# Turning half of the scan's output and half of the attention norm's state by transposing DMA reads instead of TensorE

## The chip, the cores and the metric

One Trainium2 chip, one core. The metric is the device time of one execution in microseconds, taken as the median of the runs.

## The reference

One layer of a hybrid decoder trunk over 256 tokens of width 2048: a half-step SwiGLU, a projection that feeds a gated group and a Mamba-2 scan, an output projection of both, cross-attention to 256 memory tokens, a second half-step SwiGLU and a final norm. The change touches the scan's output on its way into the output projection, and the state `h` on its way into the attention's query projection:

```python
h = h + 0.5 * swiglu(rmsnorm(h, ffn1_norm), ffn1_w_gu, ffn1_w_down)
proj = rmsnorm(h, mix_norm) @ w_in
gu, gv, z, xbc, dt_raw = split(proj)
a_out = chunked_sgu(gelu(gu), gelu(gv), gm_v_norm, gm_w_s, gm_b_s)
m_out = mamba2_group(z, xbc, dt_raw, ...)      # rmsnorm(y * silu(z), ssm_norm)
h = h + concat([a_out, m_out]) @ w_out
h = h + memory_cross_attention(rmsnorm(h, xa_norm), rmsnorm(mem, mem_norm), w_q, w_kv, w_o)
h = h + 0.5 * swiglu(rmsnorm(h, ffn2_norm), ffn2_w_gu, ffn2_w_down)
return rmsnorm(h, final_norm)
```

## The kernel before

**Products.** All large products run on TensorE as three matmuls of a split: each float32 operand becomes a rounded part `hi` and a rest `lo`, and `hi*hi`, `hi*lo`, `lo*hi` are added in PSUM. Weights arrive from HBM in blocks of 256 rows by two times 512 columns (`raw`, three buffers, L147). ACT casts a block to `hi` (L193, three buffers), DVE subtracts to `lo` (L201, two buffers). The activations are stored with features across the partitions, so that tokens have to be turned into that form first.

**Plain and summed blocks.** A plain block ("C") takes 24 matmuls of 512 columns. A summed block ("S") computes the 2 x 2 product by seven products instead of eight: 21 matmuls, for which DVE first makes four sums of the weights (`sum`, L201), ACT casts and DVE splits those too. Which block is which stands in strings such as `OUT_KINDS = "CCCCSCSC", "SCSCSCSC"`.

**The output projection** (`add_sum` with `w_out`) goes over all 16 blocks for the first two 512-column pieces of `h` (`h0`, `h1`), then over 16 blocks for the other two. In the first half blocks 0 to 5 and 7 are plain and 6 is summed, then S and C alternate from 8 to 15; in the second half blocks 0 to 3 are plain and then S and C alternate from 4. Blocks 0 to 7 multiply the gated group (`at`, `ats`), blocks 8 to 15 the scan's output (`mt`, `mts`). The scan's output has four quarters of 512 features, `c` = 0 to 3; quarter `c` gives an S piece (`mts`) and a C piece (`mt`), used by blocks 8 + 2c and 9 + 2c.

**Order.** TensorE's instructions keep the order in which the code writes them. Other work is put off with `later(fn, by)`, counted in steps, one per weight block (a C block counts as two halves). A put-off job that takes a PSUM bank is held back while summed blocks run; one marked `bankless` is not. Casts of weights stay in order among themselves on ACT, and so do the splits on DVE; a scheduler fits the other instructions between them.

**Turning on TensorE.** `m_operand(c)` scales quarter `c` of `y` by the norm's factor (L1051), one step after the other, and `mts.later` turns it a step later: per piece four transposes of 128 x 128 into a bank (`tpose`, L77). From the bank, ACT and DVE make the piece's forms: for a C piece two scaled casts on ACT (L435) and two rests on DVE (L438); for an S piece two scaled copies (`forms`, L526), three differences on DVE (L530, L532, L533), two casts (L535) and two rests (L536). `Normed.chunk(n)` does the same for the state's chunk `n` with the name `xp_xa`: all four pieces of chunks 0 and 1 are C pieces and are turned at the second half's first step.

**Turning by DMA.** Other operands of the kernel already take another way, `turn_over` (L390 to L397): ACT copies the 16-bit halves of each token row apart (`halves`), POOL's queue writes them to DRAM (`planes`), and two transposing reads on SP's queue bring 256 features by 256 tokens each into SBUF (`turned`), from where the same forms are made. With `lined=True` such a read is tied to the place between weight loads at which the code issues it (SP's queue runs in order), and both reads of a pair go at one place.

Of the kernel before, what the change touches and what calls it, by code (L numbers as in the profile page):

```python
# [34 lines left out]
KG = 4  # L35
# [4 lines left out]
C_FFN1, C_MIX, C_SSM, C_XA, C_MEM, C_FFN2 = (16 * i for i in range(6))  # L40
# [7 lines left out]
def hybrid_layer(ctx: ExitStack, tc: tile.TileContext, x, xt, mem, memt, w_gu1, w_dn1, w_in, w_s, w_out,  # L48
# [30 lines left out]
    def later(fn, by=1, bankless=False):  # L79
        put_off.append((steps[0] + by, len(put_off), fn, bankless))  # L80
# [363 lines left out]
    def operand_later(srcs, to, name, c0=None, by=1):  # L444
        def half(q):
            if q == 0:
                to.append(slot([P, KG, 2 * S], F32R, name))
            return to_operand(srcs, to[at], q, c0)

        at = len(to) + sum(1 for o in owed if o is to)  # L450
        owed.append(to)

        def first():
            owed.remove(to)
            assert len(to) == at
            half(0)
            later(lambda: half(2), by=0)

        later(first, by)

    def operand_turned(srcs, to, name, c0=None, by=(1, 4), lined=False):
        at = len(to) + sum(1 for o in owed if o is to)
        owed.append(to)

        def put(src, q):
            if q == 0:
                owed.remove(to)
                assert len(to) == at
                to.append(slot([P, KG, 2 * S], F32R, name))
            to_operand(src, to[at], q, c0)  # L470

        turn_over(srcs, by, put, lined)
# [77 lines left out]
    class Normed:  # L550
# [8 lines left out]
        def chunk(self, n, by=1):  # L559
            srcs = [h[n][:, t, :] for t in range(NT)]  # L560
            if n < 2 and not isinstance(self.xts, Pieces):
                operand_turned(srcs, self.xts, f"xt_{self.name}{n}", self.c0 + n * KG, (2.5 + 1.5 * n, 2.5))
                self.stats(n)
            elif isinstance(self.xts, Pieces):

                for i in (2 * n, 2 * n + 1):
                    later(lambda i=i: self.xts.put(i, srcs, i % 2 * KP, self.c0 + n * KG),
                          self.bys.get(i, by))
                later(lambda: self.stats(n), self.stats_by)
            else:  # L570
                operand_later(srcs, self.xts, f"xt_{self.name}{n}", self.c0 + n * KG, by)
                self.stats(n)
# [472 lines left out]
    mts = Pieces(OUT_KINDS[1], "mt")  # L1045

    def m_operand(c):
        gs = []
        for t in range(NT):
            ys = y[t][:, c * 8:c * 8 + 8, :].rearrange("p h d -> p (h d)")  # L1050
            nc.vector.tensor_scalar(out=ys, in0=ys, scalar1=rstd_m[:, t:t + 1], scalar2=None, op0=ALU.mult)  # L1051
            gs.append(ys)
        mts.later(gs, C_SSM + c * KG)

    for c in range(4):
        later(lambda c=c: m_operand(c), by=1 + c)
    na = Normed("xa", C_XA, XA_KINDS, {4: 1, 6: 1, 5: 1.5, 7: 2}, 8)

    class Both:
# [201 lines left out]
```

## Time and profile before

| what | value |
|---|---|
| median of 3 runs | 2417.68 us (2417.51 to 2418.0) |
| profiled execution, its own time | 2417.13 us |
| span of its instructions | 2415.4 us |
| mean granted TensorE clock | 0.999 |
| instructions | 29003 |
| moved by DMA | 523.80 MB, mean 217 GB/s |

A row of the timeline gives start and length in us, engine, line, operation, what it writes and reads, and how often; behind it, in brackets, the idle time of the engine before it and what ended that. Rows of a tile's view give shortest, median and longest duration in ns. A row of waits gives who waited for whom, the sum in us, how often, and the longest. Starts of consecutive matmuls tell more than their lengths, because matmuls overlap.

### The profile page before, as it was taken

Reading aid. Unit: us, or ns where it says so; the run is one execution under the profiler, and the core shown is the slowest. Engines: PE = TensorE matmul, PEld = TensorE weight load, DVE = VectorE, ACT = ScalarE, POOL = GpSimd, SP = SyncE. Lnnn points to the kernel's source line nnn. Section 1 sums busy time; section 2 is a strip of 40 time slices with the busy share of each in tenths; the row PEclk is TensorE's granted clock in tenths of the full one; section 3 lists DMA queues with packets and bytes.
Section 4 is the critical chain, followed back from the end, with each engine's and each line's share of the span. In section 5 each row is a group of like instructions: output and inputs, shape, how many; then the busy total and the mean of one; then the engine's idle time right before and its main releaser. Section 6 shows DMA issues by size and latency. Waiting matters only on the chain. (4 is left out here: it accounts for less than half of the span.)

```text
span 2415.4 us, 29003 instructions
## 1 busy us (share of the span) xinstructions
PE 2402.6 (99%) x11037; PEld 1999.1 (83%) x11037; DVE 2030.9 (84%) x1941; ACT 1385.1 (57%) x1286; POOL 85.3 (4%) x158
## 2 busy tenths in 40 slices
PE   9999999999999999999999999999999999999998
PEld 7888888888888888788888888888888888888887
DVE  8999889999877786655698988788799988999997
ACT  7566446656557664446555666655565654556554
POOL 1000000000001000000000010000000000000000
PEclk9999999999999999999999999999999999999999
DMA  8767667777757775567557677745677676677764
GB/s 307 236 220 235 207 203 232 222 225 234 242 186 215 217 227 177 202 199 227 191 192 240 230 244 226 228 157 173 201 224 232 218 223 200 219 233 222 234 219 154
DMA packets 294763, 523.80 MB, mean 217 GB/s; under 512 B 104016, under 2 KB 106096, under 8 KB 293856
## 3 DMA queue, kind: packets, MB, share of 16 engines
q1 hardware_dynamic: 283936, 485.82, 64.1%
q0 software_dynamic: 9856, 35.08, 3.9%
q8 instruction: 86, 1.41, 0.2%
q10 hardware_dynamic: 832, 1.05, 0.1%
q14 instruction: 53, 0.43, 0.0%
HBM read 476.76 MB, written 23.63 MB: 207 GB/s over the span
## 5 line engine op out<-in xcount | busy, mean ns | idle before, releaser
L201 DVE TENSOR_TENSOR lo<-raw,hi 128x2048 fp32r<-128x2048 f32 (+2 forms) x449 | 945.0, 2106 | 243.2 <-PE acc L74 170.3
L193 ACT CAST hi<-raw 128x2048 fp32r<-128x2048 f32 (+1 forms) x437 | 784.8, 1798 | 439.3 <-PE acc L74 378.9
L74 PE MATMUL acc<-hi,xp_ffn 128*128 128x512 f32 x1824 | 574.2, 389 | 0.0
L74 PEld LDWEIGHTS acc<-hi,xp_ffn 128*128 128x128 f32 x1824 | 342.4, 188 | 71.2 <-ACT hi L215 0.2
L193 ACT CAST hi<-sum 128x2048 fp32r<-128x2048 f32 x117 | 224.1, 1915 | 294.4 <-PE acc L74 148.1
L74 PE MATMUL acc<-lo,xp_ffn 128*128 128x512 f32 x912 | 355.1, 389 | 1.0 <-DVE h L682 0.9
L201 DVE TENSOR_TENSOR lo<-sum,hi 128x2048 fp32r<-128x2048 f32 x117 | 268.1, 2291 | 38.4 <-ACT hi L193 38.4
L74 PE MATMUL acc<-hi,hid 128*128 128x512 f32 x896 | 281.2, 389 | 0.0
L74 PE MATMUL acc<-hi,xt_mix 128*128 128x512 f32 x768 | 240.9, 392 | 0.0
L74 PEld LDWEIGHTS acc<-lo,xp_ffn 128*128 128x128 f32 x912 | 171.2, 188 | 37.4 <-DVE h L682 1.4
L621 DVE TENSOR_TENSOR part<-acc,part 128x512 f32<-128x512 f32 x272 | 179.9, 685 | 20.7 <-PE acc L74 7.0
L74 PEld LDWEIGHTS acc<-hi,hid 128*128 128x128 f32 x896 | 168.2, 188 | 34.9
L74 PE MATMUL acc<-lo,hid 128*128 128x512 f32 x448 | 174.3, 389 | 0.0
L74 PEld LDWEIGHTS acc<-hi,xt_mix 128*128 128x128 f32 x768 | 144.2, 188 | 30.8 <-issue 1.0
L201 DVE TENSOR_TENSOR sum<-sum,raw 128x512 f32<-128x512 f32 x234 | 161.6, 690 | 6.3
L74 PE MATMUL acc<-lo,xt_mix 128*128 128x512 f32 x384 | 149.5, 389 | 0.0
L74 PE MATMUL acc<-hi,xp_ffn1s 128*128 128x512 f32 x466 | 148.6, 389 | 0.0
L74 PE MATMUL acc<-hi,xp_ffn2s 128*128 128x512 f32 x466 | 148.6, 389 | 0.0
L201 DVE TENSOR_TENSOR sum<-raw 128x1024 f32<-128x1024 f32 x117 | 142.5, 1218 | 0.1
L74 PE MATMUL acc<-xt_mix,hi 128*128 128x512 f32 x512 | 140.1, 395 | 0.0
L74 PE MATMUL acc<-hi,hids 128*128 128x512 f32 x392 | 125.2, 389 | 0.0
L74 PE MATMUL acc<-hi,memt 128*128 128x512 f32 x384 | 121.4, 390 | 0.0
(291 smaller groups left out, 3183.3 us busy)
## 6 DMA issues: line engine op xcount, KB each, us to landing
raw<-in_w_gu SPq DMA_DIRECT2D x284, 512.0 KB, 4.6
raw<-in_w_in SPq DMA_DIRECT2D x80, 1024.0 KB, 5.2
raw<-in_w_dn SPq DMA_DIRECT2D x60, 1024.0 KB, 5.3
raw<-in_w_gu SPq DMA_DIRECT2D x136, 256.0 KB, 4.8
raw<-in_w_kv SPq DMA_DIRECT2D x24, 1024.0 KB, 5.9
raw<-in_w_out SPq DMA_DIRECT2D x21, 1024.0 KB, 5.3
planes<-halves POOLq DMA_DIRECT2D x74, 256.0 KB, 5.0
raw<-in_w_dn SPq DMA_DIRECT2D x28, 512.0 KB, 4.2
```

The costliest lines, as they stand in the source:

```text
L74: return pe(nc.tensor.matmul(out, lhsT=lhsT, rhs=rhs, start=start, stop=stop))
L193: last_cast[:] = [nc.scalar.copy(out=t[:, :n], in_=x[:, :n]).ins]
L201: last_split[:] = [nc.vector.tensor_tensor(**kw).ins]
L621: nc.vector.tensor_tensor(out=out, in0=a, in1=b, op=op)
```

## The change

Quarters 2 and 3 of the scan's output and chunks 0 and 1 of the state go the DMA's way. Their reads are tied to the order of weight loads. The four quarters are also scaled in another order of steps: 0, 2, 1, 3 at 1, 1.5, 2 and 2.5.

```diff
             if n < 2 and not isinstance(self.xts, Pieces):
                 operand_turned(srcs, self.xts, f"xt_{self.name}{n}", self.c0 + n * KG, (2.5 + 1.5 * n, 2.5))
                 self.stats(n)
+            elif n < 2 and self.name == "xa":
+                self.xts.turn_later(srcs, (5 + 1.5 * n, 1.5), self.c0 + n * KG, 2 * n, lined=True)
+                later(lambda: self.stats(n), self.stats_by)
             elif isinstance(self.xts, Pieces):
...
             gs.append(ys)
-        mts.later(gs, C_SSM + c * KG)
+        if c < 2:
+            mts.later(gs, C_SSM + c * KG)
+        else:
+            mts.turn_later(gs, (4.5, 1.4), C_SSM + c * KG, 2 * c, lined=True)

     for c in range(4):
-        later(lambda c=c: m_operand(c), by=1 + c)
+        later(lambda c=c: m_operand(c), by=(1, 2, 1.5, 2.5)[c], bankless=c > 1)
```

On TensorE, at the start of the output projection's second half, the sixteen transposes of `h0` and `h1` are gone (the groups of eight for `y` went in the same manner):

```order
 L74 MATMUL acc<-hi,at 128x512 x2
 L74 MATMUL acc<-lo,at 128x512
-L74 MATMUL acc<-hi,at 128x512
-L77 MATMUL tpose<-ident,h_90 128x128 x8
-L77 MATMUL tpose<-ident,h_91 128x128 x8
-L74 MATMUL acc<-hi,at 128x512
+L74 MATMUL acc<-hi,at 128x512 x2
 L74 MATMUL acc<-lo,at 128x512
```

The matmuls on both sides now follow each other.

On DVE, in the first half, from the sums of block 8 to the rest of block 9, there stood before only the splits of these two blocks:

```order
L201 TENSOR_TENSOR sum<-raw 128x1024
L201 TENSOR_TENSOR sum<-sum,raw 128x512 x2
L201 TENSOR_TENSOR lo<-raw,hi 128x1536
L201 TENSOR_TENSOR lo<-sum,hi 128x2048
L201 TENSOR_TENSOR lo<-raw,hi 128x2048
```

In the changed kernel the same stretch holds the last rest of quarter 2's S piece and most of quarter 3's work:

```order
L201 TENSOR_TENSOR sum<-raw 128x1024
L536 TENSOR_TENSOR mts<-forms,mts 128x512
L201 TENSOR_TENSOR sum<-sum,raw 128x512 x2
L201 TENSOR_TENSOR lo<-raw,hi 128x1536
L201 TENSOR_TENSOR lo<-sum,hi 128x2048
L530 TENSOR_TENSOR forms<-forms 128x256
L536 TENSOR_TENSOR mts<-forms,mts 128x512
L532 TENSOR_TENSOR forms<-forms 128x128
L438 SCALAR_TENSOR_TENSOR mt<-turned,col,mt 128x256
L533 TENSOR_TENSOR forms<-forms 128x128
L438 SCALAR_TENSOR_TENSOR mt<-turned,col,mt 128x256
L201 TENSOR_TENSOR lo<-raw,hi 128x2048
```

Quarter 2's other DVE work (one `mts` ahead of block 7's rest; behind it `forms`, `mt`, `forms`, `mt`, `forms`) stands just ahead of this piece. All of it stood among the sums and rests of block 6 before, with sources in PSUM (`tpose`).

On SP's queue, in the first half, the pairs of reads stand behind the loads of blocks 7 and 8:

```order
 L147 DMA raw<-in_w_out 128x512 x2
 L147 DMA raw<-in_w_out 128x2x1024
-L147 DMA raw<-in_w_out 128x2x512
-L147 DMA raw<-in_w_out 128x512 x2
+L147 DMA_TRANSPOSE turned<-planes 128x2x512 x2
+L147 DMA raw<-in_w_out 128x2x512
+L147 DMA raw<-in_w_out 128x512 x2
+L147 DMA_TRANSPOSE turned<-planes 128x2x512 x2
 L147 DMA raw<-in_w_out 128x2x1024
 L147 DMA raw<-in_w_out 128x2x512
```

The first pair fetches quarter 2, the second quarter 3. In the second half, chunk 0's pair stands behind the load of block 6 and chunk 1's behind that of block 8.

## The prediction

> **What bounds the kernel now.** I read the page's first part, then TensorE's waits over the whole span, then the timeline of the two places that the change touches.
>
> ```profile
> PE 2402.6 (99%) x11037; PEld 1999.1 (83%) x11037; DVE 2030.9 (84%) x1941; ACT 1385.1 (57%) x1286; POOL 85.3 (4%) x158
> PE acc L74 <- DVE lo L201: 1.3, 2, 0.9
> ...
> PE dt L74 <- issue: 0.5, 1, 0.5
> ```
>
> TensorE is busy for 2402.6 of 2415.4 us, and its waits, of which the first and the last of four rows stand above, sum to 4.0 us. A busy row alone proves little, because ends of matmuls are modelled, so the pitch between starts has to agree.
>
> ```profile
> 1213.05 0.39 PE L74 MATMUL acc<-hi,ats 128*128 128x512 f32 x1
> 1223.25 0.39 PE L74 MATMUL acc<-hi,mts 128*128 128x512 f32 x1
> 1228.01 0.39 PE L74 MATMUL acc<-hi,mt 128*128 128x512 f32 x1
> ```
>
> These are the first matmuls of weight blocks 6 (S, 21 matmuls), 8 (S) and 9 (C) of the output projection's first half, counted from 0; between 6 and 8 lies block 7 (C, 24 matmuls). 10.20 us over 45 and 4.76 over 21 is 0.227 us each, 5.44 for a C block, with no room for a wait. So time is TensorE's instructions at their pitch, plus whatever a change makes TensorE wait. An instruction removed from TensorE is worth its pitch; work on other engines costs nothing until a weight block's `hi` or `lo` comes late.
>
> **What the change removes.** 32 transposes leave TensorE: two groups of 8 for the scan's quarters 2 and 3, one of 16 for the state's chunks 0 and 1.
>
> ```profile
> 1200.16 0.39 PE L74 MATMUL acc<-hi,at 128*128 128x512 f32 x1
> 1200.39 1.03 PE L77 MATMUL tpose<-ident,y 128*128 128x128 f32 x8
> 1201.18 0.48 PE L74 MATMUL acc<-hi,ats 128*128 128x512 f32 x1
> 1201.49 0.40 PE L74 MATMUL acc<-lo,ats 128*128 128x512 f32 x1
> 1269.27 0.39 PE L74 MATMUL acc<-hi,at 128*128 128x512 f32 x1
> 1269.50 1.91 PE L77 MATMUL tpose<-ident,h 128*128 128x128 f32 x16
> 1271.16 0.48 PE L74 MATMUL acc<-hi,at 128*128 128x512 f32 x1
> 1271.47 0.39 PE L74 MATMUL acc<-lo,at 128*128 128x512 f32 x1
> ```
>
> From the matmul before a group to the second one behind it (the first one behind also starts its successor late) are 1201.49 - 1200.16 = 1.33 us where two pitches would be 0.45: 0.88 us for 8. In the large group it is 2.20 - 0.45 = 1.75 us for 16. Both give 0.11 us per transpose. The second group of 8 is alike, so the gain is 0.88 + 0.88 + 1.75 = **3.5 us**. Nothing else stands beside these instructions on TensorE, so all of it is on the path.
>
> The profile also shows the transposing op's own length, which is not its price here:
>
> ```profile
> L77 PE MATMUL tpose<-ident,h 128*128 128x128 f32 x80 | 10.5, 272 | 0.0
> ```
>
> The Trainium skill's page "VectorE: DVE Perf Modes", section "The three transpose paths", puts a 128x128 transpose at 390 ns on TensorE against 1309 ns through a DMA, and its rules tell the author to use TensorE where PSUM will do as the destination. Taken as prices on the path, its 390 ns would make the removal worth 12.5 us, an estimate from that page; taken as a rule, it speaks against the change. This trace disagrees with both uses: transposes overlap down to 0.11 us, and a DMA's length matters only if somebody waits for it.
>
> **What it adds off TensorE.** Each of four turn-overs needs two ACT copies into halves, two POOL writes to DRAM and two transposing reads on SP's queue.
>
> ```profile
> L390 ACT COPY halves<-gate x8: 1042/1048/1062, 1047.1 to 1098.0; 128x1024 uint16<-128x1024 uint16 x8
> planes<-halves POOLq DMA_DIRECT2D x74, 256.0 KB, 5.0
> L147 SPq DMA_TRANSPOSE turned<-planes x72: 1235/1289/4259, 61.1 to 2291.9; - x72
> turned<-planes SPq DMA_TRANSPOSE x72, 4.2
> 1186.82 2.47 DVE L1051 TENSOR_SCALAR y<-y,rstd_m 128x512 f32<-128x512 f32 x6 [0.82 <-POOL rstd_m L382]
> 1194.92 2.28 DVE L201 TENSOR_TENSOR lo<-raw,hi 128x2048 fp32r<-128x2048 f32 x1
> 1200.36 2.29 DVE L201 TENSOR_TENSOR lo<-raw,hi 128x2048 fp32r<-128x2048 f32 x1 [0.17 <-PE acc L74]
> ```
>
> ACT gains 8 x 1.05 = 8.4 us, and over the whole span it is idle for 43%; the casts behind the transposes stay, they only move. DVE's scalings of `y` come out every 0.4 us from 1186.8, quarter 2's as third and fourth, so ACT copies its halves from about 1188.2 to 1190.3, and with 5.0 us of landing and something for the issue the planes are there near 1196. SP reaches the reads behind block 7's load, which waits for block 4's `lo` (over at 1197.2 now; I allow it 0.7 more), at about 1198.4. They hold SP for 2 x 1.29 us and have landed by 1204; ACT wants them just ahead of block 7's `lo`, near 1210. Quarter 3's halves come one group later, near 1196, its planes near 1202; its reads follow block 8's load, which waits for block 5's `lo` (1202.7 now, about 1 more), near 1205, land near 1210.6 and are wanted behind block 8's sums, near 1221. I cost queue and landing at **0**: the cover is over 2 us ahead of each read and 6 us or more behind it. Gone, it would cost what the reads are late beyond it, one for one.
>
> **Where it does cost: DVE's order.** The work that turned pieces need on DVE (differences, `mts` and `mt` lows) moves from the time of the plain blocks 4 and 5, where DVE had room, to that of blocks 6 to 8, where S and C alternate and DVE is at its fullest. Its pitch is seen where it stands now, and DVE's full order without it in the rows that follow:
>
> ```profile
> 1209.31 0.41 DVE L530 TENSOR_TENSOR forms<-forms 128x256 f32<-128x256 f32 x1
> 1209.64 0.68 DVE L536 TENSOR_TENSOR mts<-forms,mts 128x512 fp32r<-128x512 f32 x1
> 1210.24 0.28 DVE L532 TENSOR_TENSOR forms<-forms 128x128 f32<-128x128 f32 x1
> 1210.44 0.47 DVE L438 SCALAR_TENSOR_TENSOR mt<-tpose,col,mt 128x256 fp32r<-128x256 f32 x1
> ...
> 1211.43 2.28 DVE L201 TENSOR_TENSOR lo<-sum,hi 128x2048 fp32r<-128x2048 f32 x1
> ...
> 1214.23 2.28 DVE L201 TENSOR_TENSOR lo<-raw,hi 128x2048 fp32r<-128x2048 f32 x1
> 1216.44 1.22 DVE L201 TENSOR_TENSOR sum<-raw 128x1024 f32<-128x1024 f32 x1
> 1217.69 1.42 DVE L201 TENSOR_TENSOR sum<-sum,raw 128x512 f32<-128x512 f32 x2
> 1219.02 1.75 DVE L201 TENSOR_TENSOR lo<-raw,hi 128x1536 fp32r<-128x1536 f32 x1
> 1221.16 2.29 DVE L201 TENSOR_TENSOR lo<-sum,hi 128x2048 fp32r<-128x2048 f32 x1 [0.39 <-ACT hi L193]
> 1223.37 2.29 DVE L201 TENSOR_TENSOR lo<-raw,hi 128x2048 fp32r<-128x2048 f32 x1
> ```
>
> By starts, the first six rows take 2.12 us; with the second `mts` (0.60, like the first) a quarter costs DVE 2.72 us. Both quarters now stand between `lo` of block 7 and `lo` of block 9, the latter quarter's last `mts` excepted. Count from the moment block 7's `lo` may start: only two such buffers exist, so it waits until block 5 is through, which is where block 6 starts, 1213.05 now and 1213.05 - 1.76 = 1211.3 without the two groups of 8. One `mts` (0.60, its cast ready at about 1211.4) stands ahead of it, so it starts at 1212.0 and DVE goes on at 1214.2. Then: quarter 2's five small ones, 0.33 + 2 x 0.40 + 2 x 0.20 = 1.53, to 1215.8; the block's first sum 1.25 (1216.44 to 1217.69) and `mts` 0.60, to 1217.6; the other sums 1.33, to 1218.9. From there to `lo<-sum` it is 2.14, with ACT's cast between: 1221.1, and on at 1223.3. Quarter 3's first six ops, 2.12, end at 1225.4, and `lo` of block 9 is ready 2.29 later, at 1227.7. TensorE needs it for the second matmul of block 9, at 1228.01 - 1.76 + 0.23 = 1226.5. **That is 1.2 us late**, and TensorE has nothing else in its order, so it waits.
>
> Behind that, DVE has 10.20 us per S and C block (4.76 + 5.44) for 8.9 us of work (1.25 + 1.33 + 1.7 + 2.2 + 2.2, with small gaps), so it makes up about 1 us per pair. Blocks 10 and 11 come within a few tenths of their need, then the distance grows again. The bounds of this term: 0, if waits overlap a bit better than the starts say; not below 0, since TensorE shows no wait in this stretch now that could go. From above, all 2 x 2.72 = 5.44 us less DVE's idle time in the two pairs, 0.97 each by a row of the next fence: 3.5 us. I take 1.2, at the place that the rows name.
>
> **The state's chunks.** Four `xp_xa` ops move behind `lo<-sum` of blocks 6 and 8 of the second half.
>
> ```profile
> 1272.43 1.66 DVE L438 SCALAR_TENSOR_TENSOR xp_xa<-tpose,col,xp_xa 128x256 fp32r<-128x256 f32 x4 [0.61 <-ACT xp_xa L435]
> 1294.56 2.29 DVE L201 TENSOR_TENSOR lo<-sum,hi 128x2048 fp32r<-128x2048 f32 x1 [0.39 <-ACT hi L193]
> 1297.82 2.29 DVE L201 TENSOR_TENSOR lo<-raw,hi 128x2048 fp32r<-128x2048 f32 x1 [0.97 <-PE acc L74]
> 1302.55 0.39 PE L74 MATMUL acc<-hi,at 128*128 128x512 f32 x1
> ```
>
> DVE is idle 0.97 us there, and `lo` of block 7 is ready at 1300.1 where the second matmul comes at 1302.8: 2.7 + 0.97 us of cover for 1.6 us. The block behind starts 0.6 us later and has that again. Cost **0**; without this cover it would be 1.6 us per chunk. Halves, write and read of `h` begin when the first half is done and have five blocks, over 24 us, for a path that took quarter 2 some 16 us.
>
> **The sum.** -3.5 + 1.2 = -2.3 us. The profiled execution took 2417.1 us (2415.4 of span and 1.7 around it), so its like would take 2414.8. The median of the runs, 2417.68, lies 0.55 above that execution; I forecast on the median: **2415.4 us**. A difference within 0.2% (4.8 us) is about what a measurement here cannot tell from no change.
>
> **Rivals.**
> - *The backlog stays hidden.* ACT's 43% idle and the blocks' cover could absorb everything: -3.5 us, 2414.2. For it: no TensorE wait anywhere in this stage now. Against it: the count above is late by 1.2 and I have found no gap in it. 0.13.
> - *DVE's backlog lands whole*, the mechanism that ends slower than before. Its place is block 9 and the blocks behind; it decides once more than 3.5 us of the 5.44 reach TensorE, and without any idle time to set against it the price is 5.44: -3.5 + 5.44 = +1.9, 2419.6. For it: 8.9 of 10.2 us are taken in each pair. Against: 0.97 us idle in each pair and the 2.7 us by which C blocks' lows come early. 0.06.
> - *SP's queue holds the weights.* A transposing read waits at its head for planes that are late, and loads queue behind it; ACT, in order too, waits with casts behind the turned pieces. To be slower by over 0.2% it must cost 4.8 + 3.5 = 8.3 us beyond its 6 us of cover, so loads or pieces must be some 14 us late: from 2422.5 up. For it: one read of 72 held SP for 4.26 us. Against: 72 such reads now, and 4.0 us of waits in all. 0.07.
> - *Transposes cost their length.* Were the 272 ns of the group's row the price, 32 would be 8.7 us and the result -8.7 + 1.2 = -7.5, 2410.2. The starts say 0.11. The page above points the same way with its 390. 0.06, which also stands for a gain that I don't see.
> - *The edit does nothing* is excluded: the order of TensorE lacks the 32 rows.
>
> **The numbers.** The forecast has 0.68. It and the hidden backlog hold 0.81: the range spans the stall's bounds, 2414.2 to 2417.7 (0 to 3.5 us), widened by 0.3 on each side for the spread of the runs: 2413.9 to 2418.0. Within 0.2%: 0.68 + 0.13 + 0.06 = 0.87; faster 0.06; slower 0.07.
>
> **What will show it.** TensorE's `tpose<-ident,y` from 32 to 16 and `h` from 80 to 64; block 9's first two matmuls about 1 us apart, released by DVE's `lo`; no wait of TensorE for a DMA or for `hi` in the stage; no stall in the second half. I am wrong if block 9 runs on time, if blocks 10 to 12 add waits of their own, or if a `raw` load is what ends a wait.

## The result and the profile after

| kernel | median, us | runs | range, us | ratio to before, 95% interval |
|---|---|---|---|---|
| before | 2417.61 | 22 | 2417.07 to 2419.91 | |
| changed | 2414.40 | 22 | 2413.87 to 2415.44 | 0.9986, 0.9980 to 0.9992 |

The changed kernel is 3.2 us faster by the medians, 0.13%, which lies within the 0.2% that the prediction called no change, and the whole interval is below 1. The prediction had 2415.4. Its profiled execution took 2414.45 us, with a span of 2412.7. The page's first part, of the changed kernel (busy time, share of the span, instructions):

```profile
PE 2399.5 (99%) x11005; PEld 1995.6 (83%) x11005; DVE 2030.5 (84%) x1941; ACT 1392.0 (58%) x1294; POOL 90.2 (4%) x166
```

TensorE has 32 instructions fewer (11037 before), ACT 8 more and POOL 8 more (the halves and the writes of their planes). The groups of the transposed tiles show which are gone. The first row is of the kernel before, where `h` had 80; the other two are of the changed kernel:

```profile
L77 PE MATMUL tpose<-ident,y x32: 270/272/328, 1187.4 to 1207.5; 128*128 128x128 f32 x32
L77 PE MATMUL tpose<-ident,h x64: 270/272/273, 701.2 to 1732.5; 128*128 128x128 f32 x64
L77 PE MATMUL tpose<-ident,y x16: 270/272/328, 1187.9 to 1195.3; 128*128 128x128 f32 x16
```

TensorE's waits over the span, of the changed kernel (in total, times, longest; the first of four rows). Before, this row had 1.3 us in two waits:

```profile
PE acc L74 <- DVE lo L201: 1.6, 4, 1.0
```

The longest of the four is new, and TensorE's timeline has it at the start of block 9:

```profile
1226.72 0.39 PE L74 MATMUL acc<-hi,mt 128*128 128x512 f32 x1
1228.16 0.50 PE L74 MATMUL acc<-lo,mt 128*128 128x512 f32 x1 [1.05 <-DVE lo L201]
1228.50 0.62 PE L74 MATMUL acc<-hi,mt 128*128 128x512 f32 x2
```

Read it by starts: two steps take 1.78 us where two pitches of 0.227 would be 0.45, so the wait costs 1.33 us; the bracket shows only what is left idle behind a matmul whose own 0.39 us run out. DVE's timeline of the same stretch, of the changed kernel, says why:

```profile
1212.56 2.28 DVE L201 TENSOR_TENSOR lo<-raw,hi 128x2048 fp32r<-128x2048 f32 x1
1214.76 0.42 DVE L530 TENSOR_TENSOR forms<-forms 128x256 f32<-128x256 f32 x1
...
1216.29 1.22 DVE L201 TENSOR_TENSOR sum<-raw 128x1024 f32<-128x1024 f32 x1
1217.42 0.69 DVE L536 TENSOR_TENSOR mts<-forms,mts 128x512 fp32r<-128x512 f32 x1
...
1221.47 2.29 DVE L201 TENSOR_TENSOR lo<-sum,hi 128x2048 fp32r<-128x2048 f32 x1 [0.37 <-ACT hi L193]
1223.68 0.42 DVE L530 TENSOR_TENSOR forms<-forms 128x256 f32<-128x256 f32 x1
...
1225.82 2.28 DVE L201 TENSOR_TENSOR lo<-raw,hi 128x2048 fp32r<-128x2048 f32 x1
```

From block 7's `lo` (first row) to block 9's (last row) DVE has one gap, the 0.37 us in which ACT casts the sums. Quarter 2's small work stands from 1214.76 to 1216.29, quarter 3's from 1223.68 to 1225.82. Block 9's `lo` ends at 1228.10; its matmul would have come at 1226.95.

SP's queue of the changed kernel shows how long the two pairs of reads held it:

```profile
1198.88 5.83 SPq L147 DMA_TRANSPOSE turned<-planes  x2
...
1206.43 4.96 SPq L147 DMA_TRANSPOSE turned<-planes  x2
```

The two reads of quarter 2 landed at 1205.8 and 1206.7. ACT took up the first of these pieces at 1210.36 and the second at 1211.82, and waited for neither.

To see where the time went, every matmul of the changed trace was set beside the same matmul of the trace before, and their starts subtracted. The changed trace is 0.5 us behind until block 4, picked up at waits in the first 85 us; this part differs by up to 0.7 us among the three traces of the kernel before. From there:

| place | change, us |
|---|---|
| two groups of 8 transposes gone | -0.88 and -0.88 |
| block 9 waits for `lo` | +1.32 |
| group of 16 transposes gone | -1.75 |
| a wait of the query's projection, at 1430 | -0.80 |
| a wait at 1474 | -0.23 |

With the 0.5 us of the start the rows give -2.7 us, the difference of the two spans. The first three rows are the prediction's sum, -2.2 us for its -2.3. The last two stand in a part of the kernel that the change doesn't touch. The first of them, in timelines of SP's queue, ACT and TensorE of the kernel before:

```profile
1419.05 2.58 SPq L147 DMA_TRANSPOSE turned<-planes  x2
1425.60 0.62 ACT L429 CAST qt<-turned 128x512 fp32r<-128x512 f32 x1 [0.89 <-DMA turned<-planes]
1430.81 0.50 PE L74 MATMUL acc<-lo,xp_xa 128*128 128x512 f32 x1 [0.86 <-DVE lo L201]
```

and of the changed kernel:

```profile
1417.36 2.58 SPq L147 DMA_TRANSPOSE turned<-planes  x2
1422.91 0.62 ACT L429 CAST qt<-turned 128x512 fp32r<-128x512 f32 x1 [0.98 <-DMA turned<-planes]
1428.36 0.50 PE L74 MATMUL acc<-lo,xp_xa 128*128 128x512 f32 x1
```

ACT waits for the second of two transposing reads: 6.55 us after the pair was issued before, 5.55 us with the change. Behind this cast stand ACT's `hi`, DVE's `lo` and TensorE, which waits 1.02 us before and 0.27 after (by starts).

### The profile page after: what moved, and what is told of

Same layout as the page of the kernel before. It is cut to its first block, busy times and chain, and to the rows that moved or that the text cites. A ratio compares the mean times of both kernels' runs of the same rounds, so it can differ in the third digit from the quotient of the medians.

```text
span 2412.7 us, 28971 instructions
## 1 busy us (share of the span) xinstructions
PE 2399.5 (99%) x11005; PEld 1995.6 (83%) x11005; DVE 2030.5 (84%) x1941; ACT 1392.0 (58%) x1294; POOL 90.2 (4%) x166
```

## The experiments

The theory: transposes are worth 0.11 us each, the DMAs and ACT's and POOL's work cost nothing, and the one cost is DVE's order at block 9. Rivals: SP's queue, another owner of the wait, and a gain that isn't the transposes'.

**The changed kernel again**, for the spread between chips.

> The changed kernel itself, for a second trace and as the measure of the others. Theory (a transpose is worth 0.11 us, and DVE's order makes block 9 of the output projection's first half late): TensorE gains 3.5 us and loses 1.3 us between the first two matmuls of block 9, so 2.2 us net up to the end of the output projection; whatever else differs, the two short waits in the attention's projections above all, hangs on when DMAs land and should differ between two runs of one kernel. Rival (these two waits shrink because of the change): they come out at the small lengths again, about 0.3 and 0.4 us above a pitch where the kernel before had 1.0 and 0.6.

Median 2414.51 us (11 runs, 2414.11 to 2414.71) beside 2417.45 of before; ratio 0.9987, 0.9978 to 0.9996. Its trace has block 9's wait (+1.31), as the theory says, and the shorter wait at 1430 (0.26) once more, as the rival says.

**The scan's quarters alone.** The state's chunks go by TensorE as before.

```diff
-            elif n < 2 and self.name == "xa":
-                self.xts.turn_later(srcs, (5 + 1.5 * n, 1.5), self.c0 + n * KG, 2 * n, lined=True)
-                later(lambda: self.stats(n), self.stats_by)
```

> Only the scan's quarters 2 and 3 go by DMA; the state's chunks are turned on TensorE as before. Theory: 16 transposes less give 1.76 us, block 9 is late by 1.3 us as in the full change, so 0.4 to 0.5 us net: hardly faster than before, 1.7 us slower than the full change. Rival (a transpose costs its own length of 0.27 us): 4.3 - 1.3 = 3 us faster than before. Rival (the reads or planes, not DVE's order, make block 9 late): the wait at block 9 is ended by a DMA.

Median 2415.60 us (2415.36 to 2416.20), ratio 0.9992, 0.9983 to 1.0001. Against the trace before: -0.88, -0.88, +1.30 at block 9, nothing in the second half, -0.75 at 1430. So the stage gives the theory's 0.4 to 0.5 us, and the wait at 1430, which the theory did not have, gives more than that. The medians lie 1.85 us below the kernel before, of which the trace explains 1.2; the interval still holds no change at all.

**The state's chunks alone.** The quarters go by TensorE as before.

```diff
-        if c < 2:
-            mts.later(gs, C_SSM + c * KG)
-        else:
-            mts.turn_later(gs, (4.5, 1.4), C_SSM + c * KG, 2 * c, lined=True)
+        mts.later(gs, C_SSM + c * KG)
...
-        later(lambda c=c: m_operand(c), by=(1, 2, 1.5, 2.5)[c], bankless=c > 1)
+        later(lambda c=c: m_operand(c), by=1 + c)
```

> Only the state's chunks 0 and 1 go by DMA; the scan's quarters are turned on TensorE as before. Theory: 16 transposes less give 1.7 us and nothing is late: block 9 on pitch, no wait in the second half; 1.7 us faster than before, half a microsecond slower than the full change. Rival (DVE is as full in the second half, and the four xp_xa operations make a C block late): a wait of up to 1 us at block 7 or 9 of the second half.

Median 2414.58 us (2413.88 to 2415.49), ratio 0.9988, 0.9979 to 0.9997: as fast as the whole change. In the trace -1.8 at the group of 16, no wait at block 9 or in the second half, and again 0.26 instead of 1.02 at 1430. The profiled execution took 2415.49, the slowest of the eleven: two waits for `lo`, at 1450.7 and 1453.3, cost it 0.46 and 0.43 by starts, which the trace of the changed kernel does not have there. So the quarters' turn-over keeps little: 1.76 us saved, 1.3 given back at block 9.

**Quarter 2 fetched and put earlier**, so that its DVE work stands among blocks 4 to 6.

```diff
-            mts.turn_later(gs, (4.5, 1.4), C_SSM + c * KG, 2 * c, lined=True)
+            mts.turn_later(gs, (3 if c == 2 else 4.5, 1.4), C_SSM + c * KG, 2 * c, lined=True)
```

> The full change with quarter 2 fetched at 3 steps behind its scaling instead of 4.5, so that its DVE work stands ahead of the sums of block 6 and only quarter 3's stands between blocks 7 and 9. Theory: block 7's rest starts at its buffer's release again, the rest of block 9 is ready about 1.7 us before TensorE wants it, no wait: 3.5 us faster than before, 1.3 us faster than the full change. Rival (the reads are what makes block 9 late): quarter 3's reads stand where they stood, so the wait stays at 1.3 us and the time is that of the full change.

Median 2414.94 us (2414.23 to 2415.43), ratio 0.9988, 0.9979 to 0.9997: not faster than the whole change. The wait didn't vanish but was split, as ACT's and TensorE's timelines of this kernel show:

```profile
1204.17 0.91 ACT L526 ACTIVATE forms<-turned,col 128x256 f32<-128x256 f32 x2 [2.94 <-DMA planes<-halves]
1212.44 0.50 PE L74 MATMUL acc<-lo,ats 128*128 128x512 f32 x1 [0.23 <-DVE lo L201]
1215.05 0.50 PE L74 MATMUL acc<-lo,ats 128*128 128x512 f32 x1 [0.25 <-DVE lo L201]
1228.52 0.50 PE L74 MATMUL acc<-lo,mt 128*128 128x512 f32 x1 [0.27 <-DVE lo L201]
```

By starts block 9 is late by 0.54 instead of 1.32, but block 6 is late twice, by 0.50 and 0.53: 1.57 in all. Its sums came late because ACT's first cast of quarter 2 (first row) waited 2.94 us, and not for a read: `halves`, `turned` and `forms` share a ring of six buffers, and at this time `forms` took a buffer of quarter 3's `halves`, which POOL's write had not yet emptied (the bracket names that write). The theory of DVE's order had not counted this wait.

**Quarter 3 put one S and C pair later**, behind block 10 instead of block 8.

```diff
-            mts.turn_later(gs, (4.5, 1.4), C_SSM + c * KG, 2 * c, lined=True)
+            mts.turn_later(gs, (4.5, 1.4 if c == 2 else 3.4), C_SSM + c * KG, 2 * c, lined=True)
```

> Quarter 3's turned pieces are put one S and C pair later (a distance of 3.4 blocks behind their reads instead of 1.4), so that its DVE work of 2.7 us stands behind the `lo<-sum` of block 10; quarter 2's stays as in the changed kernel. Theory (DVE's order makes block 9's `lo` late, because both quarters' work stands ahead of it): DVE goes on at the `lo` of block 9 some 2.1 us earlier than in the changed kernel, so its 1.05 us wait there is gone, and the `lo` of block 11 comes 0 to 0.3 us late instead: about 1.0 to 1.3 us faster than the changed kernel, so 2413.1 to 2413.5 beside 2414.5. Rival 1 (the wait belongs to quarter 2's work and to block 7's late start, not to quarter 3's): a wait of about 1 us stays at block 9, and the time is 2414.5 as before this edit. Rival 2 (the backlog only moves): block 11's first two matmuls stand 1 us or more apart, and the time is 2414.2 to 2414.7.

Median 2414.00 us (11 runs, 2413.39 to 2414.36) beside 2417.37, ratio 0.9985, 0.9976 to 0.9994. TensorE's timeline of this kernel, at blocks 9 and 11:

```profile
1226.50 0.39 PE L74 MATMUL acc<-hi,mt 128*128 128x512 f32 x1
1226.73 0.39 PE L74 MATMUL acc<-lo,mt 128*128 128x512 f32 x1
...
1236.70 0.39 PE L74 MATMUL acc<-hi,mt 128*128 128x512 f32 x1
1237.35 0.50 PE L74 MATMUL acc<-lo,mt 128*128 128x512 f32 x1 [0.26 <-DVE lo L201]
```

Block 9 is on time, one pitch between its first two matmuls: the wait belonged to both quarters' work ahead of it, as the theory says. Block 11 is 0.53 late by starts and block 14's sums another 0.3, more than the 0 to 0.3 expected, so the traces give 0.5 us and not 1.0 to 1.3.

**The reads at once behind their writes**, three weight blocks' loads earlier on SP's queue, the pieces where they were.

```diff
-            mts.turn_later(gs, (4.5, 1.4), C_SSM + c * KG, 2 * c, lined=True)
+            mts.turn_later(gs, (1, 4.9), C_SSM + c * KG, 2 * c, lined=True)
```

> The transposing reads of the scan's quarters 2 and 3 are put on SP's queue at once behind their planes' writes (a distance of 1 instead of 4.5 blocks), the pieces where they were. So SP reaches the reads before their planes are in memory. Theory of the queue (what the prediction had as a rival, and priced at 0 for the changed kernel because the reads stand behind two weight loads): SP stands at the first read until the planes have landed, some 5 us, and the weight loads behind it go out that much later; with the 2 to 4 us by which these loads come early in the changed kernel, TensorE waits 1 to 4 us at one or two of the blocks 6 to 9, and the time is 2415.5 to 2418.5. Rival (the queue has cover for that as well): loads land later, but no wait of TensorE is ended by a DMA or by `hi`, block 9's 1.05 us wait is as it was, and the time is 2414.5 within 0.4.

Median 2423.25 us (10 runs, 2421.83 to 2423.87), ratio 1.0023, 1.0014 to 1.0032: the theory of the queue, and almost 5 us beyond its range. Timelines of this kernel:

```profile
1196.26 0.53 SPq L147 DMA_DIRECT2D raw<-in_w_out  x1
1204.22 2.57 SPq L147 DMA_TRANSPOSE turned<-planes  x2
1213.75 1.47 ACT L193 CAST hi<-raw 128x1536 fp32r<-128x1536 f32 x1 [7.85 <-DMA raw<-in_w_out]
1215.28 0.50 PE L74 MATMUL acc<-hi,ats 128*128 128x512 f32 x1 [1.49 <-ACT hi L193]
1218.18 0.79 PE L74 MATMUL acc<-lo,ats 128*128 128x512 f32 x1 [2.40 <-DVE lo L201]
1218.77 1.05 PE L74 MATMUL acc<-hi,ats 128*128 128x512 f32 x2
```

SP stands before quarter 3's read from 1196.8 to 1204.2, until its planes are in memory. Block 6's load goes out behind it at 1206.89, where the changed kernel has it at 1192.84, as block 5's goes out behind quarter 2's reads at 1196.26 (the first row) instead of 1184.81. ACT gets block 6's weights after 7.85 us of nothing, and TensorE waits at blocks 5 and 6. Then comes what neither theory had priced: behind the waits the pitch is not 0.227 us. Busy times by stretches of this kernel (after the engines: granted TensorE clock, DMA share, GB/s):

```profile
1213.00:1216.00 3.00, 1.29 (x5) 0.51 (x3) 2.16 (x3) 1.47 (x1) 0.00 (x0) 1.00 1.01 395
1216.00:1220.00 4.00, 1.82 (x4) 1.49 (x5) 3.70 (x3) 3.51 (x2) 0.00 (x0) 0.65 0.72 218
1220.00:1224.00 4.00, 4.00 (x11) 3.08 (x10) 4.00 (x6) 3.79 (x7) 0.00 (x0) 0.50 0.62 236
1224.00:1230.00 6.00, 6.00 (x28) 4.96 (x27) 5.75 (x9) 2.42 (x2) 0.00 (x0) 1.00 0.55 177
```

The granted clock falls to 0.50 until 1224, and matmuls start 0.43 us apart. The 0.65 is a mean: 1.2 us of that stretch at 1.00 and 2.8 at 0.50, so the clock fell at about 1217.2. By starts, the waits at blocks 5 and 6 cost 6.0 us, the slow matmuls 2.8, block 9 another 1.0, where the changed kernel has 1.3 at block 9 alone.

**The kernel before, twice more**, for the wait at 1430.

> The kernel before once more, for its trace: the first trace of it has two waits in the attention part, 1.0 us at 1430 and 0.6 us at 1474, which in every trace with the change are 0.26 and 0.2 to 0.6. If they belong to the kernel before (theory), they stand here again within 0.3 us, and some 0.8 to 1 us of what the change saves lies there, outside its own stage. If they come from how long that execution's transposing reads took to land (rival), the wait at 1430 is 0.3 here, and the time of this execution is about 2416.6 to 2417.0.

> The same kernel a third time, for a second sample of these two waits: theory 1.0 and 0.6 us again, rival 0.3 us at 1430, or one time the one and one time the other.

2417.77 and 2418.42 us. The wait at 1430 is 1.12 us in both by starts (1.02 in the first trace), the one at 1474 is 0.39 and 0.51 (0.62). So the first belongs to the kernel before, in 3 of 3 traces, against 0.26 or 0.27 in all 7 traces of the changed kernel and its variants so far; the second wanders from run to run. What in the change shortens a wait so far behind it was the question of two kernels more. Both start from the kernel before and leave its 32 transposes in place.

**Two buffers of the shared ring passed over**, so that later turned pieces lie elsewhere.

```diff
         mts.later(gs, C_SSM + c * KG)
+        if c == 3:
+            for i in range(2):
+                spare = half_k(F32, "spare")
+                nc.gpsimd.memset(spare[:, :8], 0.0)
```

> The kernel before, with two more buffers taken from the ring of six that `turned` and `halves` use, each only set to zero in 8 columns by POOL, behind the scaling of quarter 3: later turned pieces stand two buffers further on, as they do with either half of the change. No DMA, no transpose and no other work is added. The question is the 1.0 to 1.1 us wait of TensorE at 1430, which all three traces of the kernel before have and no trace with a part of the change (0.27). Theory A (it hangs on which buffer the query's turned pieces land in): the wait is 0.3 here, and the time is 0.8 us shorter. Theory B (it hangs on what went through SP's queue before, four or eight reads more): the wait stays at 1.0 to 1.1.

**The quarters' turn-overs as well, and nobody reads them**, with the ring brought back to where it was.

```diff
         mts.later(gs, C_SSM + c * KG)
+        if c > 1:
+            turn_over(gs, (4.5, 1.4), lambda to, q: None, lined=True)
+            for i in range(2):
+                spare = half_k(F32, "spare")
+                nc.gpsimd.memset(spare[:, :8], 0.0)
```

> The kernel before, with the two turn-overs of the scan's quarters 2 and 3 done as well (halves, writes, four transposing reads), which nobody uses: TensorE keeps its 32 transposes. Four more buffers of the ring are passed over, so that later pieces stand in the same buffers as in the kernel before. Theory B (the wait at 1430 hangs on what went through SP's queue): it is 0.3 here. Theory A (it hangs on the buffer): it stays at 1.0 to 1.1. If it stays in both of these kernels, neither is the cause. In the stage itself the extra reads cost nothing by the prediction's reckoning of SP, ACT and POOL (0 for all of them): no wait of TensorE between 1190 and 1270 beyond 0.15 us; a rival, by which ACT's four copies or the reads delay a weight block, has a wait of 0.3 us or more at one of the blocks 6 to 9.

Timelines of SP's queue, ACT and TensorE; the kernel with two buffers passed over:

```profile
1419.71 2.58 SPq L147 DMA_TRANSPOSE turned<-planes  x2
1426.32 0.62 ACT L429 CAST qt<-turned 128x512 fp32r<-128x512 f32 x1 [0.81 <-DMA turned<-planes]
1431.53 0.50 PE L74 MATMUL acc<-lo,xp_xa 128*128 128x512 f32 x1 [0.93 <-DVE lo L201]
```

and the kernel with the extra turn-overs:

```profile
1418.94 2.58 SPq L147 DMA_TRANSPOSE turned<-planes  x2
1424.47 0.61 ACT L429 CAST qt<-turned 128x512 fp32r<-128x512 f32 x1
1429.95 0.50 PE L74 MATMUL acc<-lo,xp_xa 128*128 128x512 f32 x1
```

Other buffers leave the wait as it was (6.6 us to the second cast, 2417.43 us). The extra turn-overs, which save TensorE nothing, take most of it away: 5.5 us to the cast, 0.75 us won at 1430, 2416.06 us in one run. So these 0.75 us are no gain of the transposes; they come with turn-overs earlier in the program. Whether their copies, writes or reads do it, no run separates. Why a later pair of reads then lands 1 us sooner stays open. In the stage itself the extra copies, writes and reads cost nothing: from 82 to 1430 us every matmul stands where it stands in the kernel before, within 0.12 us.

**Quarter 3 late, and the differences on POOL.** Three operations of each turned S piece move from DVE to POOL.

```diff
-            in_turn(ps, last_split, lambda: nc.vector.tensor_tensor(
-                out=b[:, 0:2], in0=a[:, 1:2].broadcast_to([P, 2, P]), in1=a[:, 0:4:3], op=ALU.subtract), c0)
+            eng = nc.gpsimd if in_sbuf and self.name == "mt" else nc.vector
...
-            nc.vector.tensor_tensor(out=b[:, 2], in0=a[:, 0], in1=b[:, 1], op=ALU.subtract)
-            nc.vector.tensor_tensor(out=b[:, 3], in0=a[:, 2], in1=b[:, 2], op=ALU.subtract)
+            eng.tensor_tensor(out=b[:, 2], in0=a[:, 0], in1=b[:, 1], op=ALU.subtract)
+            eng.tensor_tensor(out=b[:, 3], in0=a[:, 2], in1=b[:, 2], op=ALU.subtract)
```

> As the run with quarter 3's pieces put 3.4 blocks behind their reads, and the three differences `forms<-forms` of each of the two turned quarters made on POOL instead of DVE. That takes 0.33 + 0.20 + 0.20 = 0.73 us per quarter off DVE; quarter 3's second `mts` (0.60) moves ahead of block 11's `lo`. Theory (what TensorE still waits for at blocks 11 and 14, 0.53 + 0.34 us in that run's trace, is DVE's full order there and nothing else): neither wait is left, all 3.5 us of the transposes are kept, and the time is 0.6 to 0.9 us below that run's 2414.0, so 2413.1 to 2413.4. Rival 1 (the chain gets longer: ACT's cast of the differences waits for POOL, DVE's second `mts` for that cast, and the weights' `lo` stands behind it): DVE is idle for over 0.7 us ahead of a second `mts`, the waits stay or move to block 8 or 9, 2414 to 2415.5. Rival 2 (the waits come from ACT's `hi` casts or from loads): the waits stay as they are, 2414.0.

Median 2418.79 us (11 runs, 2417.24 to 2420.06), ratio 1.0005, 0.9996 to 1.0014: rival 1, worse than it was priced. Timelines of its POOL, ACT, DVE and TensorE:

```profile
1212.30 2.55 DVE L201 TENSOR_TENSOR lo<-raw,hi 128x2048 fp32r<-128x2048 f32 x1
1212.78 2.39 POOL L536 TENSOR_TENSOR forms<-forms 128x128 f32<-128x128 f32 x1
...
1232.29 1.99 POOL L532 TENSOR_TENSOR forms<-forms 128x256 f32<-128x256 f32 x1 [17.12 <-ACT forms L526]
1234.35 0.79 POOL L535 TENSOR_TENSOR forms<-forms 128x128 f32<-128x128 f32 x1
1235.71 0.62 ACT L538 CAST mts<-forms 128x512 fp32r<-128x512 f32 x1 [2.64 <-POOL forms L536]
1236.36 0.69 DVE L539 TENSOR_TENSOR mts<-forms,mts 128x512 fp32r<-128x512 f32 x1 [1.54 <-ACT mts L538]
1238.58 0.50 PE L74 MATMUL acc<-hi,mt 128*128 128x512 f32 x1 [1.28 <-ACT hi L193]
1240.91 0.50 PE L74 MATMUL acc<-lo,mt 128*128 128x512 f32 x1 [1.83 <-DVE lo L201]
```

POOL needs 3.4 to 4.1 us for the three, where DVE took 0.73. ACT's cast waits 2.64 us for them and DVE 1.54 for the cast; block 11's `hi` stands behind the one and its `lo` behind the other, so TensorE gets both late. Work taken off a full engine has come back as a wait in the order of two others. The profiled execution is the fastest of the eleven; nine of the others list a mean granted clock of 0.998 where it has 0.999, so they may have lost the clock behind these waits, which no trace shows.

**Quarter 3's S piece late, its C piece last**, all on DVE. The distance now differs between the two pieces of a quarter.

```diff
-            later(lambda: put(to.rearrange("p (k s) -> p k s", k=KP), q), by=by[1], bankless=True)
+            later(lambda: put(to.rearrange("p (k s) -> p k s", k=KP), q), by=by[1 + q // 2 if len(by) > 2 else 1],
+                  bankless=True)
...
-            mts.turn_later(gs, (4.5, 1.4), C_SSM + c * KG, 2 * c, lined=True)
+            mts.turn_later(gs, (4.5, 1.4) if c == 2 else (4.5, 3.4, 7.4), C_SSM + c * KG, 2 * c, lined=True)
```

> As the run with quarter 3's pieces put 3.4 blocks behind their reads, all differences on DVE, but only quarter 3's S piece stands there (1.9 us of DVE); its C piece (two `mt` lows, 0.8 us) is put 7.4 blocks behind the read, so that it stands behind the `lo<-sum` of block 14, the last but one, ahead of block 15 that uses it. Theory (DVE's order alone; a wait goes where the work ahead of a `lo` exceeds its cover): in that run block 11's `lo` was 0.42 us late with 0.8 us of C work and 1.33 us of S work ahead of it, so it comes in time here; block 14's `lo<-sum` was 0.16 late behind waits of 0.53, and without these waits and the 0.8 us of C work it is late by 0.16 + 0.53 - 0.8, that is not at all. TensorE then has no wait over 0.15 us from block 6 to 15, the trace lies 0.8 to 0.9 us ahead of that run's behind this stage, and the time is 2413.0 to 2413.4. Rival (the C work moves the wait on): block 15's `lo` or the second half's first `lo` comes late by 0.3 us or more, and the time is 2413.6 to 2414.4.

Median 2413.14 us (11 runs, 2412.64 to 2413.84) beside 2417.75, ratio 0.9981, 0.9972 to 0.9990: the theory's number. DVE's and TensorE's timelines of this kernel:

```profile
1227.11 0.39 PE L74 MATMUL acc<-hi,mt 128*128 128x512 f32 x1
1227.34 0.39 PE L74 MATMUL acc<-lo,mt 128*128 128x512 f32 x1
...
1251.55 2.29 DVE L201 TENSOR_TENSOR lo<-sum,hi 128x2048 fp32r<-128x2048 f32 x1 [0.39 <-ACT hi L193]
1253.75 0.88 DVE L439 SCALAR_TENSOR_TENSOR mt<-turned,col,mt 128x256 fp32r<-128x256 f32 x2
1253.89 0.50 PE L74 MATMUL acc<-lo,mts 128*128 128x512 f32 x1
```

Blocks 9 and 11 are on time. Of all waits between 1190 and 1270, 0.13 us is left, at block 14, where the sums' `lo` comes just in time; the C piece's two lows stand behind it and delay nobody. This kernel is faster than both: by 4.6 us against the runs of the kernel before beside it, and by 1.3 us against the changed kernel's 2414.40. That last step rests on runs taken at different times, whose intervals overlap (0.9972 to 0.9990 and 0.9980 to 0.9992); the traces give it as 1.32 - 0.13 = 1.2 us.

## Why the prediction was nearly right

- **The transposes, -3.5: right.** 0.88, 0.88 and 1.75 us, each found at its place, alone in the two partial kernels and together in the whole. The 272 ns of the duration row are not their price on TensorE. The 390 ns that the prediction takes from the Trainium skill's page "VectorE: DVE Perf Modes" stand there for bf16, and these transposes are of float32.
- **DMA, ACT, POOL and SP at 0: right.** The extra turn-overs without the gain moved no matmul of the stage. The sizes on the way were too kind: a pair held SP for 5.83 and 4.96 us, not for 2 x 1.29, and quarter 2's reads landed at 1205.8 and 1206.7, not by 1204, which left 4.6 and 5.1 us of cover instead of 6. The cover that the prediction named is what did it: with the reads moved ahead of three blocks' loads, the time rose by 8.7 us (2423.25 against 2414.51). The rival "SP's queue holds the weights" was a true mechanism, kept away by the reads' place behind these loads. Its price, 8.3 us for loads some 14 us late, is close to this run, where block 6's load goes out 14.05 us later; but 2.8 us of the loss are the halved clock, which the prediction's "one for one" did not have.
- **Block 9 late by 1.2: right.** 1.32 by starts, released by DVE's `lo`, and DVE's rows come out as counted, each within 0.2 us once 0.5 us of the start is taken off. Putting quarter 3 later removes it; leaving the quarters out removes it.
- **Blocks 10 to 12 and the second half at 0: right.** No wait of TensorE there in the changed kernel.
- **The sum, -2.3 on 2417.68: 1 us short.** The step that failed is the one behind "sum to 4.0 us": the waits outside the stage were read as fixed. One of them, at 1430, has 0.8 us that goes with either half of the change, and also with turn-overs that nobody uses. It could not have been worked out from the trace of before, which doesn't show on what the landing of those reads depends; a bound for it could, since the row with two waits and 1.3 us was there. By the number alone the rival "the backlog stays hidden" (2414.2) is nearer to the measured 2414.40 than the forecast (2415.4), and that is chance: block 9's wait, which this rival denies, is there with 1.32 us, and the shorter waits at 1430 and 1474, which neither had, give 1.03 us of it back.

## What to carry to other kernels

A full engine's order is a schedule: count when each piece on it is needed, and put what can wait behind the operation that can't. The same 5.4 us of DVE work cost 1.3 us when it stood in one place, and 0.13 when its parts stood just ahead of their own users. Before an operation is moved to an idle engine, count the chain through every queue in order behind it; and put a DMA that waits for data behind the loads that others wait for.

## What the runs showed of the hardware that was not expected

- TensorE at half clock after waits: in the kernel with the early reads, with 1.49 and 2.40 us of idle time around one matmul, the granted clock was 0.50 from about 1217.2 to 1224, for 6.8 us. It fell 3.4 us after the first of the two waits began (1213.8). The Trainium skill's page "TensorE: Matmul & The Clock Gate", section "Why this matters for your kernels", warns of gaps above some 3 us. The trace agrees if the two waits count as one gap. The 1.28 and 1.83 us in the kernel with POOL, also around one matmul, left the clock at 1.00 in the profiled execution, and so did the 1 us at block 9.
- POOL beside DVE: with DVE idle, POOL's 128x256 difference took 0.74 us and its 128x128 one 0.46, where DVE's rows have 0.42 and 0.28, so 1.8 and 1.6 times as long (the profile calls its spans on POOL rough); beside a `lo` or `lo<-sum` of DVE the same two took 1.99 and 2.39 us, and one such `lo` took 2.55 instead of 2.28. The Trainium skill's page "GPSIMD Engine Reference" has GpSimd about 2 times slower on two inputs (section "Engine selection") and says that it shares its SBUF interfaces with VectorE (section "Specifications"). The first agrees with POOL alone; the second agrees too, and here it is the larger part.
- The pair of reads behind the wait at 1430 has landed 6.5 to 6.6 us after its issue in the four traces without extra turn-overs, and 4.7 to 5.8 us after it in the ten with two or four of them, some 130 to 220 us earlier in the program. The cause is open.
